# Where the cast of a weight chunk stands in ScalarE's queue at the seams of a two-block network

## The chip, the cores and the metric

One core of one Trainium2 chip. The time is the device time of one execution in microseconds (us); several runs of a kernel are taken and their median stands for it. The profile is of one execution, and its span leaves out a little of what the device time holds.

## The reference

256 tokens of width 1024, in float32, pass through a first block (one layer: a mixer of four branches, a feed-forward) and then a second block of two layers. What matters here is the second block:

```python
def swiglu_ffn(h, w_up, w_down):
    a, b = jnp.split(h @ w_up, 2, axis=-1)
    return (jax.nn.silu(a) * b) @ w_down
...
    for l in range(DEPTH_2):
        x = x + 0.5 * swiglu_ffn(rmsnorm(x, ffn1_norm[l]), ffn1_w_up[l], ffn1_w_down[l])
        x = x + mixer(rmsnorm(x, mix_norm[l]), w_in[l], b_in[l], ..., w_out[l], cos, sin)
        x = x + 0.5 * swiglu_ffn(rmsnorm(x, ffn2_norm[l]), ffn2_w_up[l], ffn2_w_down[l])
        x = rmsnorm(x, final_norm[l])
    return x
```

The feed-forward's hidden width is 2816. The mixer projects its normed input (gated convolution, queries, keys and values, gates), runs windowed attention and a convolution of 31 taps, and projects their gated sum back with w_out. A *seam* below is a place where a part has added its result to x and the next part starts with a norm of x: three seams follow a feed-forward's down projection, two follow w_out.

## The kernel before

**Layout.** Activations lie transposed, 128 channels on the partitions and the 256 tokens along the free axis. The residual x is four tiles `X[0]` to `X[3]`, each a pair of 128-channel columns. Every float32 operand of a matmul is split in two float32r parts: a high half, which is a copy rounded by a cast, and a low half, which is the rest. A product is three matmuls: high by high, high by low, low by high.

**Weights come in chunks** of 128 x 2048 (1 MB; 8 blocks of 128 input channels for a pair of output columns). A down projection has 22 blocks, so each column pair takes chunks of 8, 8 and 6; w_out, the gated convolution (glu) and the up projections take one chunk of 8 for each. `weights(name, i, c0)` fetches a chunk and those after it in a fixed order, up to `ahead` chunks ahead: SP loads the raw chunk (L189), ScalarE casts it to the high half (L195), VectorE subtracts to get the low half (L197). There are two buffers for raw chunks, three for high and three for low halves. TensorE reads the halves in `mm_pair` (L269): a full chunk is 48 matmuls of 256 columns, one of 6 blocks is 36. `mm` sets `ahead` to 2 before each call; its parameter `hold`, which would set it to 1 for the last chunk of a product, is not used by any caller.

**The seam.** After column pair j of a down projection or of w_out, VectorE adds the product to `X[j]` (L482 or L738), and `after(j)` feeds the pair into the next norm. `Norm.feed` multiplies each of the two columns by the norm's gain into its high half on ScalarE (L388, in `split`), takes the low half on VectorE (L389), squares x on ScalarE (L397) and adds the squares on VectorE (L398). At the seam from layer 0 to layer 1 the norm before (`pre`) is applied in the same feed: one more square and two more multiplications (L423) come first. The factor that the norm needs from the sum of squares is multiplied in later (`Norm.done`: a column sum on TensorE in L351, a reciprocal root in small VectorE operations, a broadcast), so the next product's matmuls can start with the column pairs that are there: the first chunk after the seam uses pair 0 first and pair 3 last.

**Order.** The program is traced in the order of the Python code. A planner then puts the instructions of each engine in a fixed queue when the program is built, by its own estimate of when each becomes ready and by their order in the trace; `high_priority` moves a part of the trace forward in that order. Buffers of one name (a tag) are shared, and an instruction that writes a new tile waits for a free one. `issue_after(ins)` ties what it encloses on `ins`'s engine behind `ins` in the queue, without a wait for its end.

Other names in the rows: `mm` is a PSUM tile of a product, `xs` holds the halves of the normed input, `slot` is an arena buffer (the hidden tile of a feed-forward among others), `pc` is the column sum. In the mixer, `zsq` (L579) and `ra` (L594) are tiles of one tag (`t2`, four buffers) around the queries and keys: the code asks for the square of a projected half in its turn, and for `ra` after the last square of a group of heads, with raised priority. Each `ra` is a product of one such half and a table. L683 are the convolution's taps.

Of the kernel before, what the change touches and what calls it, by code (L numbers as in the profile page):

```python
# [1 line left out]

# [1 line left out]

# [16 lines left out]
KD = D // P  # L21
# [111 lines left out]
class Builder:  # L133
    def __init__(self, ctx, tc, dram):
        self.tc, self.nc, self.d, self.ctx = tc, tc.nc, dram, ctx
        pool = lambda n, b=1, **kw: ctx.enter_context(tc.tile_pool(name=n, bufs=b, **kw))
        self.p_raw = pool("raw", 2)
        self.p_hi = pool("hi", 3)
        self.p_lo = pool("lo", 3)
        self.con = pool("con")  # L140
        self.st = pool("st")
        self.ar = pool("ar")
        self.tp = pool("tmp", 2)
        ps = bass.MemoryType.PSUM
        self.p_mm = pool("pmm", 3, space=ps)
        self.p_park = pool("park", 1, space=bass.MemoryType.DRAM)
        self.parked, self.parking = {}, iter(())
        self.p_sm = pool("psm", 1, space=ps)
        self.p_sc = pool("psc", 3, space=ps)
        self.p_y = pool("py", 1, space=ps)  # L150
        self.queue, self.ready = [], {}
        self.twice, self.later = False, iter(())
        self.next_ = 0
        self.ahead = 2
        nc = self.nc
        self.ones = self.con.tile([P, P], F32, name="ones")
        nc.vector.memset(self.ones, 1.0)
        self.eps = self.con.tile([P, 16], F32, name="eps")
        nc.vector.memset(self.eps, EPS)
        self.eps = self.eps[:, :1]  # L160
        self.ident = self.con.tile([P, P], F32, name="ident")
        self.X = [self.st.tile([P, 2, NT], F32, name=f"x{j}") for j in range(4)]
# [6 lines left out]
    def weights(self, name, i, c0=0, first=None):  # L169
        key = (name, i, c0)  # L170
        while key not in self.ready or self.next_ < min(self.ready[key][2] + 1 + self.ahead, len(self.queue)):
            n, ii, cc, w, how = self.queue[self.next_]
            nc = self.nc
            r = self.p_raw.tile([P, CH], F32, name="raw")
            by = (BY_QKV if n[:3] == "qkv" else BY) // 4
            h = self.p_hi.tile([P, CH + 64], F32R, name="hi")[:, by:by + CH]
            lo = self.p_lo.tile([P, CH + 64], F32R, name="lo")[:, by:by + CH]
            if self.next_ < 2:
                for j in range(4):
                    c = slice(j * 512, (j + 1) * 512)  # L180
                    if self.next_ == 0:
                        first(j)
                    nc.sync.dma_start(r[:, c], self.d[n][ii, :, c])
                    nc.scalar.copy(h[:, c], r[:, c])
                    nc.vector.tensor_sub(lo[:, c], r[:, c], h[:, c].bitcast(F32))
                self.ready[n, ii, cc] = (h, lo, self.next_)
                self.next_ += 1
                continue
            nc.sync.dma_start(r[:, :w], self.d[n][ii, :, cc:cc + w])  # L189
            if how == 1:  # L190
                nc.sync.dma_start(lo.bitcast(F32)[:, :w], self.parked[n, ii])
            if how == 2:
                nc.scalar.mul(lo[:, :w], r[:, :w], -1.0)
                nc.gpsimd.dma_start(lo[:, :w], self.d[n][ii, :, cc:cc + w], accum_op=ALU.add)
            self.cast = nc.scalar.copy(h[:, :w], r[:, :w]).ins  # L195
            if how == 0:
                nc.vector.tensor_sub(lo[:, :w], r[:, :w], h[:, :w].bitcast(F32))  # L197
            self.ready[n, ii, cc] = (h, lo, self.next_)
            self.next_ += 1
        h, lo, _ = self.ready[key]  # L200
        next(self.parking, None)
        return h, lo
# [179 lines left out]
    def split(self, src, H, L, gain=None):  # L382
        nc = self.nc
        if gain is None:
            nc.scalar.copy(H, src)  # L385
            return nc.vector.tensor_sub(L, src, H.bitcast(F32))  # L386
        else:
            nc.scalar.mul(H, src, gain)  # L388
            return nc.vector.scalar_tensor_tensor(L, src, gain, H.bitcast(F32), op0=ALU.mult, op1=ALU.subtract)  # L389

    def sumsq(self, acc, x, tag="sqa", bufs=1):
# [16 lines left out]
    class Norm:  # L408
# [6 lines left out]
        def feed(self, j, sums=True):  # L415
            b = self.b
            if j == 0:
                self.H, self.L = b.new_xs()
            x = b.X[j]
            if self.pre:  # L420
                self.acc0 = b.sumsq(self.acc0, x, "zq", 6)
                for i in range(2):
                    b.nc.scalar.mul(x[:, i], x[:, i], b.prm(self.pre, 2 * j + i))  # L423
            for i in range(2):
                k = 2 * j + i
                ins = b.split(x[:, i], self.H[k], self.L[k], b.prm(self.gain, k))
            if sums:
                self.acc = b.sumsq(self.acc, x)
            return ins

# [26 lines left out]
    def ffn(self, l, n, norm, after, duo=False):  # L457
        nc = self.nc
        nk = DFF2 // P
        hid = [self.slot(i, [P, 4, NT], F32R) for i in range((nk + 1) // 2)]  # L460
        H = [hid[k // 2][:, k % 2] for k in range(nk)]
        L = [hid[k // 2][:, 2 + k % 2] for k in range(nk)]
        for m, pt in self.mms(f"{n}u{l}", nk, norm.H, norm.L, duo):
            if m == 0:
                norm.done(duo)
            z = self.t2("z")
            nc.vector.tensor_mul(z, pt, norm.rb2)  # L467
            s = self.t1("s")
            ins = nc.scalar.activation(s, z[:, 0], AF.Silu)
            if m == 4:  # L470
                self.mark = ins.ins
            f = self.t1("f")
            nc.vector.tensor_mul(f, s, z[:, 1])  # L473
            if m == 3:
                self.parking, self.later = self.later, iter(())
            self.split(f, H[m], L[m])
        for j in range(4):
            pt = self.mm(f"{n}d{l}", j, nk, H, L)
            if n == "ffn2" and l == NL - 1 and j == 3:
                after(j, pt)  # L480
                break
            nc.vector.scalar_tensor_tensor(self.X[j], pt, 0.5, self.X[j], op0=ALU.mult, op1=ALU.add)  # L482
            after(j)
# [18 lines left out]
    def mixer(self, l, norm, after):  # L502
        nc = self.nc
        H, L = norm.H, norm.L
# [22 lines left out]
        for m in range(8):  # L527
            pt = self.mm(f"glu{l}", m, KD, H, L)
# [21 lines left out]
        for c in QKV:  # L550
# [4 lines left out]
            for hf in range(2):  # L555
                h, lo = self.weights(f"qkv{l}", 2 * c + hf)
                for j in range(2):
                    for i in range(4):
                        k = hf * 4 + i
                        js = slice(j * P, (j + 1) * P)  # L560
                        w = slice(i * 512, (i + 1) * 512)
# [172 lines left out]
                nc.vector.tensor_add(g[:, 0], g[:, 0], g[:, 1])  # L734
                self.split(g[:, 0], MH[m], ML[m])
        for j in range(4):
            pt = self.mm(f"out{l}", j, KD, MH, ML)
            nc.vector.tensor_add(self.X[j], pt, self.X[j])  # L738
            after(j)

# [587 lines left out]
```

## Time and profile before

| | |
|---|---|
| device time, median of 3 runs | 1812.47 us (1810.83 to 1815.7) |
| the profiled execution: device time | 1818.6 us |
| its span | 1816.7 us |
| TensorE busy | 1765.8 us, 97% |
| VectorE busy | 1390.5 us, 77% |
| ScalarE busy | 932.3 us, 51% |
| GpSimd busy | 84.1 us, 5% |
| mean granted TensorE clock | 0.984 |

Times in rows are us from the start of the span. Engines: PE is TensorE's matmuls, PEld its weight loads, DVE is VectorE, ACT is ScalarE, POOL is GpSimd, SP issues loads. A timeline row shows start, duration, engine, line, operation, output<-inputs, shapes and count (consecutive equal instructions are merged), and in brackets the idle time of the engine before it with what ended it. The granted clock is a share of 2.4 GHz; 0.50 is 1.2 GHz.

### The profile page before, as it was taken

What the parts mean: (1) busy time and instruction counts of PE and PEld (TensorE: products, weight loads), DVE (VectorE), ACT (ScalarE), POOL (GpSimd) and SP (SyncE); (2) the same over time, 40 slices, a digit from 0 to 9 for tenths busy, and PEclk for the clock granted to TensorE, in tenths of its full rate; (3) what the DMA queues carried; (4) which work ended last, traced back from release to release, by engine and by line L of the source; (5) the groups of instructions that cost most, each with busy time, mean ns of one, the idle gap of its engine ahead of it and who ended that gap; (6) DMA issues with size and microseconds to landing.
All of it is one profiled execution on the core that took longest, in us unless ns stands there. A gap on an engine that the chain in (4) does not pass through costs nothing.

```text
span 1816.7 us, 33703 instructions
## 1 busy us (share of the span) xinstructions
PE 1765.8 (97%) x14048; PEld 1694.6 (93%) x14048; DVE 1390.5 (77%) x2137; ACT 932.3 (51%) x1134; POOL 84.1 (5%) x156
## 2 busy tenths in 40 slices
PE   7999999999999999999999999999999999999998
PEld 7989899999999898888999999999998888999997
DVE  7886878656776699998877766777689998776653
ACT  4354455444555454467645555555444456654443
POOL 0000000000011100000000110011300000000000
PEclk9999999999999999999999998999989999999999
DMA  7425447773788758875458986688757774455552
GB/s 280 173 94 209 159 146 272 270 266 135 269 305 302 250 188 295 286 259 141 169 180 276 304 295 218 223 299 299 273 195 286 282 274 142 163 186 186 186 183 96
DMA packets 79560, 409.34 MB, mean 225 GB/s; under 512 B 9905, under 2 KB 10033, under 8 KB 40241
## 3 DMA queue, kind: packets, MB, share of 16 engines
q1 hardware_dynamic: 51552, 339.07, 53.9%
q0 software_dynamic: 10000, 35.66, 5.8%
q10 hardware_dynamic: 17856, 32.48, 4.9%
q8 instruction: 110, 1.80, 0.4%
q14 instruction: 42, 0.34, 0.1%
HBM read 375.71 MB, written 31.46 MB: 224 GB/s over the span
## 4 chain that ended last, share of the span: by engine, by line
PE 48%; DVE 19%; issue 17%; DMA 6%; ACT 5%; POOL 2%; ACTq 0%; POOLq 0%; DVEq 0%
PE mm L269 37%; DVE lo L197 7%; ACT hi L195 3%; DVE spare L683 2%; DMA raw<-ffn1d 2%; DVE slot L683 2%; PE mm L292 1%; PE mm L564 1%; PE mm L562 1%; PE mm L563 1%; PE y L646 1%; DMA raw<-out 1%; POOL qkv L217 1%; DMA raw<-glu 1%; DMA raw<-ffn1u 1%
## 5 line engine op out<-in xcount | busy, mean ns | idle before, releaser
L269 PE MATMUL mm<-xs,hi 128*128 128x256 f32 x5440 | 974.0, 282 | 18.4 <-ACT xs L388 8.6
L269 PEld LDWEIGHTS mm<-xs,hi 128*128 128x128 f32 x5440 | 831.4, 190 | 26.4 <-ACT xs L388 9.2
L195 ACT CAST hi<-raw 128x2048 fp32r<-128x2048 f32 (+1 forms) x288 | 542.6, 1885 | 504.5 <-PE mm L269 235.5
L197 DVE TENSOR_TENSOR lo<-raw,hi 128x2048 fp32r<-128x2048 f32 (+1 forms) x254 | 573.6, 2259 | 292.4 <-ACT hi L195 291.5
L269 PE MATMUL mm<-xs,lo 128*128 128x256 f32 x2720 | 738.7, 282 | 5.8 <-DVE lo L197 5.3
L269 PEld LDWEIGHTS mm<-xs,lo 128*128 128x128 f32 x2720 | 504.6, 190 | 9.4 <-DVE lo L197 6.3
L269 PE MATMUL mm<-slot,hi 128*128 128x256 f32 x2304 | 399.7, 278 | 4.1 <-DVE slot L1010 2.4
L269 PEld LDWEIGHTS mm<-slot,hi 128*128 128x128 f32 x2304 | 345.2, 188 | 5.1 <-DVE slot L1010 2.8
L269 PE MATMUL mm<-slot,lo 128*128 128x256 f32 x1152 | 306.0, 278 | 0.0
L269 PEld LDWEIGHTS mm<-slot,lo 128*128 128x128 f32 x1152 | 209.8, 188 | 0.0
L683 DVE SCALAR_TENSOR_TENSOR slot<-slot,prm,slot 128x256 f32<-128x256 f32 x360 | 149.3, 479 | 0.0
L385 ACT CAST slot<-f 128x256 fp32r<-128x256 f32 (+1 forms) x104 | 45.3, 439 | 159.4 <-DVE f L473 156.9
L562 PE MATMUL mm<-hi,xs 128*128 128x512 f32 x288 | 113.1, 393 | 0.0
L563 PE MATMUL mm<-lo,xs 128*128 128x512 f32 x288 | 113.1, 393 | 0.0
L564 PE MATMUL mm<-hi,xs 128*128 128x512 f32 x288 | 112.6, 391 | 0.0
L562 PEld LDWEIGHTS mm<-hi,xs 128*128 128x128 f32 x288 | 54.1, 188 | 11.0
L467 DVE TENSOR_TENSOR z<-mm,rb 128x512 f32<-128x512 f32 x88 | 60.2, 688 | 5.4 <-ACT rb L379 1.3
L563 PEld LDWEIGHTS mm<-lo,xs 128*128 128x128 f32 x288 | 54.1, 188 | 11.0
L216 DVE TENSOR_TENSOR slot<-slot 128x512 fp32r<-128x512 f32 x96 | 63.9, 685 | 0.5 <-ACT slot L215 0.5
L564 PEld LDWEIGHTS mm<-hi,xs 128*128 128x128 f32 x288 | 54.1, 188 | 11.0
L386 DVE TENSOR_TENSOR slot<-f,slot 128x256 fp32r<-128x256 f32 (+1 forms) x104 | 47.7, 462 | 15.0 <-ACT slot L385 14.8
L215 ACT CAST slot<-slot 128x512 fp32r<-128x512 f32 x96 | 56.5, 610 | 0.0
(283 smaller groups left out, 1422.4 us busy)
## 6 DMA issues: line engine op xcount, KB each, us to landing
raw<-ffn1u SPq DMA_DIRECT2D x44, 1024.0 KB, 5.1
raw<-ffn2u SPq DMA_DIRECT2D x44, 1024.0 KB, 4.8
raw<-qkv SPq DMA_DIRECT2D x36, 1024.0 KB, 6.5
raw<-win SPq DMA_DIRECT2D x24, 1024.0 KB, 4.8
lo<-qkv SPq DMA_DIRECT2D x18, 1024.0 KB, 6.8
raw<-wup SPq DMA_DIRECT2D x16, 1024.0 KB, 4.8
raw<-wdown SPq DMA_DIRECT2D x16, 1024.0 KB, 6.1
raw<-ffn1d SPq DMA_DIRECT2D x16, 1024.0 KB, 6.8
```

Source lines behind the costliest of these rows:

```text
L195: self.cast = nc.scalar.copy(h[:, :w], r[:, :w]).ins
L197: nc.vector.tensor_sub(lo[:, :w], r[:, :w], h[:, :w].bitcast(F32))
L215: nc.scalar.copy(h, r)
L216: nc.vector.tensor_sub(r.bitcast(F32R), r, h.bitcast(F32))
L269: nc.tensor.matmul(pt[:, m], w[:, i, c], x[k], start=first and m == 0 and i == 0 and j == 0, stop=last and i == n - 1 and j == 2, skip_gro ...
L385: nc.scalar.copy(H, src)
L386: return nc.vector.tensor_sub(L, src, H.bitcast(F32))
L467: nc.vector.tensor_mul(z, pt, norm.rb2)
L562: nc.tensor.matmul(pz[j], H[k][:, js], h[:, w], start=k == 0, stop=False)
L563: nc.tensor.matmul(pz[j], H[k][:, js], lo[:, w], start=False, stop=False)
L564: nc.tensor.matmul(pz[j], L[k][:, js], h[:, w], start=False, stop=k == 7)
L683: nc.vector.scalar_tensor_tensor(acc[i], u, w, acc[i], op0=ALU.mult, op1=ALU.add)
```

## The change

At the last chunk of the last column pair (j = 3) of each down projection of the second block and of w_out, `mm` now gets `hold`, so that this call of `weights` runs one chunk ahead and not two. The chunk that it leaves out is then traced by the next call, that of the first chunk behind the seam, which also traces the one after it. `split` notes its last multiplication, `Norm.feed` hands it on at j = 3, and the next cast that `weights` traces is tied behind it in ScalarE's queue; the casts after that one are not tied.

```diff
@@ Builder.__init__
         self.queue, self.ready = [], {}
+        self.fed = None
@@ Builder.weights
-            self.cast = nc.scalar.copy(h[:, :w], r[:, :w]).ins
+            with self.tc.issue_after(self.fed) if self.fed else nullcontext():
+                self.cast = nc.scalar.copy(h[:, :w], r[:, :w]).ins
+            self.fed = None
@@ Builder.split
-            nc.scalar.mul(H, src, gain)
+            self.fed_ = nc.scalar.mul(H, src, gain).ins
@@ Builder.Norm.feed
             if sums:
+                if j == 3:
+                    b.fed = b.fed_
                 self.acc = b.sumsq(self.acc, x)
@@ Builder.ffn
         for j in range(4):
-            pt = self.mm(f"{n}d{l}", j, nk, H, L)
+            pt = self.mm(f"{n}d{l}", j, nk, H, L, j == 3)
@@ Builder.mixer
         for j in range(4):
-            pt = self.mm(f"out{l}", j, KD, MH, ML)
+            pt = self.mm(f"out{l}", j, KD, MH, ML, j == 3)
```

## Rows read from the trace of the kernel before

**Rows 1.** The page, busy us of each engine (share of the span), instructions:

```profile
PE 1765.8 (97%) x14048; PEld 1694.6 (93%) x14048; DVE 1390.5 (77%) x2137; ACT 932.3 (51%) x1134; POOL 84.1 (5%) x156
```

**Rows 2.** Timeline of ScalarE around the seam at 623 us:

```profile
619.28 1.92 ACT L195 CAST hi<-raw 128x2048 fp32r<-128x2048 f32 x1 [1.97 <-DMA raw<-glu]
627.87 1.90 ACT L195 CAST hi<-raw 128x2048 fp32r<-128x2048 f32 x1 [6.67 <-DMA raw<-glu]
629.67 0.90 ACT L388 ACTIVATE xs<-x,prm 128x256 fp32r<-128x256 f32 x2
630.48 0.61 ACT L397 ACTIVATE sq<-x 128x512 f32<-128x512 f32 x1
```

**Rows 3.** Timeline of VectorE around the same seam:

```profile
623.68 0.68 DVE L482 SCALAR_TENSOR_TENSOR x<-mm,x 128x512 f32<-128x512 f32 x1
629.79 2.29 DVE L197 TENSOR_TENSOR lo<-raw,hi 128x2048 fp32r<-128x2048 f32 x1 [5.43 <-ACT hi L195]
632.00 0.88 DVE L389 SCALAR_TENSOR_TENSOR xs<-x,prm,xs 128x256 fp32r<-128x256 f32 x2
```

**Rows 4.** Timeline of TensorE around the same seam:

```profile
626.35 0.40 PE L269 MATMUL mm<-xs,hi 128*128 128x256 f32 x2
...
626.70 0.40 PE L269 MATMUL mm<-xs,hi 128*128 128x256 f32 x2
...
630.23 1.01 PE L269 MATMUL mm<-xs,hi 128*128 128x256 f32 x3 [3.01 <-ACT xs L388]
...
632.54 0.58 PE L269 MATMUL mm<-xs,hi 128*128 128x256 f32 x1 [1.09 <-DVE xs L389]
```

**Rows 5.** Timeline of ScalarE at the seams at 929 and 1119 us:

```profile
929.62 1.91 ACT L195 CAST hi<-raw 128x2048 fp32r<-128x2048 f32 x1 [2.36 <-PE mm L269]
...
1119.52 1.91 ACT L195 CAST hi<-raw 128x2048 fp32r<-128x2048 f32 x1 [2.24 <-DMA raw<-ffn1u]
```

**Rows 6.** Windows: stretch, length, PE busy (instructions), granted clock, DMA share, GB/s:

```profile
629.60:639.80 10.20, 8.48 (x38) 0.50 0.30 103
...
sum 30.70, PE 26.98; mean PE 8.99
```

**Rows 7.** Windows of 22 us from the first matmul behind a seam:

```profile
622.85:644.85 22.00, 17.90 (x119) 0.77 0.49 178
1312.61:1334.61 22.00, 17.97 (x121) 0.77 0.58 200
1116.35:1138.35 22.00, 19.28 (x123) 0.77 0.52 187
929.38:951.38 22.00, 21.68 (x184) 1.00 0.55 188
```

**Rows 8.** Timeline of TensorE at the seams at 1119 and 1314 us:

```profile
1123.34 0.62 PE L269 MATMUL mm<-xs,hi 128*128 128x256 f32 x3 [2.63 <-ACT xs L388]
...
1319.91 1.01 PE L269 MATMUL mm<-xs,hi 128*128 128x256 f32 x3 [2.94 <-ACT xs L388]
```

**Rows 9.** Timeline of VectorE in the mixer, queries and keys:

```profile
692.81 4.44 DVE L683 SCALAR_TENSOR_TENSOR slot<-slot,prm,slot 128x256 f32<-128x256 f32 x11
...
702.47 0.68 DVE L594 TENSOR_TENSOR ra<-zq,slot 128x512 f32<-128x512 f32 x1
```

**Rows 10.** Timeline of ScalarE in the same stretch:

```profile
689.22 0.63 ACT L579 ACTIVATE zsq<-zq 128x512 f32<-128x512 f32 x1 [4.13 <-DVE zq L576]
...
702.48 0.62 ACT L579 ACTIVATE zsq<-zq 128x512 f32<-128x512 f32 x1
```

**Rows 11.** Timeline of TensorE behind the seam at 929 us:

```profile
935.70 0.95 PE L351 MATMUL pc<-ones,sqa 128*128 128x1 f32 x8
```

**Rows 12.** Windows: a stretch of TensorE behind another wait:

```profile
908.00:918.00 10.00, 9.15 (x79) 1.00 0.50 194
```

**Rows 13.** The page, DMA issues: KB each, median us to landing:

```profile
raw<-ffn2u SPq DMA_DIRECT2D x44, 1024.0 KB, 4.8
```

**Rows 14.** The chain that ended last, 600 to 660 us:

```profile
621.59 6.18 DMA raw<-glu
```

More of the change, by code (lines that the diff above doesn't have):

```diff
@@ L1 @@
-from contextlib import ExitStack
+from contextlib import ExitStack, nullcontext
 import numpy as np
```

## Prediction

> **What bounds the kernel now.** I read the page first: TensorE is busy for 97% of the span [rows 1], so only its idle time and its slow clock can be won. The list of waits names what it waits for longest inside the second block: the scaled copy of the residual that ScalarE writes in line 388. The timeline finds three such waits, all at the seams from a feed-forward to what follows (near 623, 1119 and 1314 us); the two seams after the mixer (near 929 and 1618) have the same code without such a wait.
>
> Call the last chunk before a seam C0, the next ones C1 to C5, and E the end of C0's matmuls. ScalarE runs its instructions in the order in which they were queued, and at all five seams the cast of C3 is queued ahead of the feed of the last column pair. At 623 us that cast had to wait 6.67 us for its load, so the two feed multiplications ran at 629.67 [rows 2], although their input, the sum of line 482, was there at 624.36 [rows 3]. TensorE had run 36 matmuls of C1 on the three older pairs, stopped, got the first half of the feed at 630.23 and waited once more, 1.09 us, for line 389 [rows 4], which stood on VectorE behind the subtraction of the same C3 [rows 3]. At 1119 us the cast waited 2.24 us for its load. At 929 its data had come, the feed was late by the cast alone (1.9 us), and 36 matmuls, three of which take 0.35 us, covered that with 4.2 us [rows 4, 5].
>
> The second half of the price is the clock. Behind each of the three long waits the granted clock is 0.50 (1.2 GHz) for 10.2 to 10.3 us, 30.7 in all [rows 6].
>
> **What the three seams cost.** The windows of 22 us from the first matmul of C1 hold 119, 121 and 123 matmuls at the disturbed seams and 184 at the other two, of which one is shown [rows 7]. Short by 65, 63 and 61, at 0.117 us: 7.6 + 7.4 + 7.1 = 22.1 us. Of it 3.01 + 1.09 at the first, 2.94 + the same 1.09 at 1319 and 2.63 are waiting, 10.8 in all [rows 4, 8]; the rest, 11.3, is the clock.
>
> The Trainium skill (TensorE: Matmul & The Clock Gate, section HAM oscillation) charges half of the throttled time: by it 30.7 us would cost 15.3, and with the waits, less the 3.7 us of them that lie inside the slow stretches, the seams would cost 22.4. That hardly differs from the count, and the sum stands on the count.
>
> **The change, part by part.** With hold, the last call for weights of C0 fetches C1 only. The load, cast and subtraction of C2 are then traced behind the feed, and its cast alone is tied behind the feed's last multiplication. This happens five times; at the sixth place (the last feed-forward) no chunk is left and nothing is fed.
>
> *The load of C2* sits on SP, which has loads alone here. It is not tied and needs a raw buffer that C0's subtraction has freed: it goes out as before, and before E its data had come (its cast ran at 619.28 at the first seam [rows 2]). Cost nothing; if something stood ahead of it on SP, that thing's length.
>
> *The cast of C3*, the one that blocks today, is not tied at all. Whether it moves depends on whether its hi buffer may be handed out before C2's, which is asked for earlier. The trace says it may not. The product of line 594 had its operand, as the square of it at 689.22 shows, and a raised priority, yet VectorE ran eleven convolution taps from 692.81 and began it at 702.47, when ScalarE began the square that had asked for a buffer of that tag one place earlier [rows 9, 10]. So I take the buffers of a tag as given in program order: C3 follows C2, and C2 follows the feed.
>
> *The feed* then follows the sum at once: sum 0.68 [rows 3], two multiplications 0.90, the square 0.61 [rows 2]. The high halves are there at E + 1.6, the low ones (0.88 for two [rows 3]) a little later, before TensorE's E + 4.2, and ScalarE is free at E + 2.2. All of the 10.8 us of waiting, and with it the clock's fall, should go. At 1119 the feed has one more square and two more multiplications, as long as these: high halves at E + 3.1, low ones by E + 3.6, still in time.
>
> *What is late next: C2.* Cast from E + 2.2, 1.91 us [rows 5], subtraction 2.29 [rows 3]: done at E + 6.4, at 1119 at E + 7.9. TensorE ends C1 at E + 5.6 (48 matmuls) and wants the low half with C2's third matmul, E + 5.7; the column sum of line 351 (0.95) can run in between, as it is now near that place [rows 11]. Bounds: nothing where the column sum comes first (C2 is then wanted at E + 6.6), 0.7 where it doesn't; I take 0.3 at four seams, 1.2 in all. At 1119 the bounds are 1.2 and 2.2; taken 1.2, since the sum of the older squares can fill the rest. Does such a short wait drop the clock? The nearest row is a stretch of 10 us from 908, in which TensorE is idle for 0.85 and the granted clock stays at 1.00 [rows 12]. I take no clock cost; the other end is the 4.5 us that the clock cost at 1119 (7.1 less 2.63), for each seam.
>
> *C4's load* waits for C2's raw buffer, which is freed at E + 6.4 instead of about E. 4.8 us for a load [rows 13], cast and subtraction 4.2: E + 15.4, wanted at E + 6.6 + 2 x 5.6 = E + 17.8. The 2.4 us to spare hide it: nothing. POOL's queue is not passed.
>
> Sum: 22.1 - 1.2 - 1.2 = 19.7 us. The profiled execution, 1818.6 us, becomes 1798.9. It is 6.1 above the median of the runs shown, and I take the seams to be the same in all: 1812.5 - 19.7 = **1792.8 us**.
>
> **The rivals.** *C4 starves.* The loads of C4 and C5 now start 2.3 us apart, and a load that overlapped with the next one took 6.18 us [rows 14], not 4.8. That eats 1.4 of the 2.4 us, and one more subtraction (2.29) ahead of C4's on VectorE makes it 1.3 late: at five seams 6.5, so 1799. Against it: the load of C3 today overlaps in the same way and only its cast's place hurts. The Trainium skill (DMA: Bandwidth & Descriptors, section Issuing engines are not separate DMA queues) says that transfers in flight interleave on the same sixteen engines. By that both loads of the pair would be late by up to the length of the overlap; the 6.18 us agrees.
>
> *The change doesn't do what it says.* If buffers are not given in order, C3's cast stays ahead of the feed and C2's comes behind both. The three waits stay. At a mixer seam C2's subtraction then queues behind C3's (to 933.9), the feed's halves and sum (1.4) and ends at 937.5, when TensorE wants it at 935.2 to 936: 1.5 to 2.3 us twice, 1816; with the clock's fall there too, 1825. Against it stands the order of lines 594 and 579 [rows 9, 10], though these are of another tag with four buffers.
>
> *Slower, by C2.* The wait for C2's low half takes the place of the one for the feed at all five seams, and takes the clock with it. From there it decides: five times 4.5 and my 2.4 of waiting are 24.9 against 22.1, so 1815; if the waits reach the 2.6 us that cost the clock today, five times 7.1 = 35.5, so 1826. For it: the waits I left in the sum. Against it: the 0.85 us after 908 that cost no clock, and that nothing ready before E + 4.1 stands ahead of the subtraction on VectorE. The Trainium skill (TensorE: Matmul & The Clock Gate, section A second HAM failure mode) tells of a kernel whose clock swung through micro-idles alone. By that the 1815 would come true; no row here shows it.
>
> **How the numbers follow.** My sum as told: 0.74, with 1789 to 1798 as its own range (residual waits of nothing, or of 0.7 four times, 2.2 once and the clock at one seam, within the runs' scatter). C4 starves: 0.10. No effect at the feed: 0.09. C2 takes the wait's place: 0.07. The range 1787 to 1805 holds the first but for surprises and most of the second: about 0.81. The three runs before lie 4.9 us apart, so 0.3% (5.4 us) is about what a measurement can tell from no change. Faster: 0.74, and 0.07 of the starved case. Same: its other 0.03 and 0.04 of no effect. Slower: 0.05 of no effect and the last case's 0.07.
>
> **What would show it.** On ScalarE at each seam: feed, square, cast, cast, in this order, the feed within 1 us of the sum. No wait of TensorE for line 388; granted clock 1.00 through all five; 175 or more matmuls in each of the five windows. Right in kind but mis-sized: a wait for line 197 at E + 5.7, or for a load at E + 18. Wrong: a cast still ahead of the feed, or the clock at 0.50 behind a new wait.

## The result, and the profile after

| | before | after |
|---|---|---|
| device time, median of 4 runs each, same chip | 1811.65 us (1809.67 to 1815.7) | 1796.64 us (1792.25 to 1799.7) |
| ratio, 95% interval | | 0.9893 (0.987 to 0.9916) |
| the profiled execution: device time / span | 1818.6 / 1816.7 us | 1799.7 / 1797.9 us |
| mean granted TensorE clock | 0.984 | 0.994 |

The kernel became faster by 0.84% to 1.3%. On the 1812.5 us that the prediction started from, the interval is 1788.9 to 1797.2 us; forecast were 1792.8. The profiled executions lie 18.9 us apart; the prediction's sum was 19.7, from 1818.6 to 1798.9.

The page's line of the engines (busy us, share of the span, instructions), which answers to [rows 1]:

```profile
PE 1753.4 (98%) x14048; PEld 1682.8 (94%) x14048; DVE 1386.3 (77%) x2137; ACT 932.4 (52%) x1134; POOL 83.5 (5%) x156
```

TensorE's busy time fell by 12.4 us with the same instructions: matmuls that run at half clock are longer. The rest of the gain is idle time.

Seams keep the names of their times in the kernel before; behind the change they come earlier. Lines have moved: the cast is L197, the low half's subtraction L200, the matmul L272, the column sum L354, the broadcast L376, the feed L391 and L392, its square L400, the added squares L401, the sums L487 and L743. The timeline of ScalarE at the seam near 623 us, against [rows 2]:

```profile
623.22 0.91 ACT L391 ACTIVATE xs<-x,prm 128x256 fp32r<-128x256 f32 x2 [3.21 <-DVE x L487]
624.04 0.62 ACT L400 ACTIVATE sq<-x 128x512 f32<-128x512 f32 x1
624.56 1.90 ACT L197 CAST hi<-raw 128x2048 fp32r<-128x2048 f32 x1
628.80 1.90 ACT L197 CAST hi<-raw 128x2048 fp32r<-128x2048 f32 x1 [2.35 <-DMA raw<-glu]
```

Feed, square, C2's cast, C3's cast: so it stands at all five seams. VectorE there, against [rows 3]:

```profile
622.50 0.69 DVE L487 SCALAR_TENSOR_TENSOR x<-mm,x 128x512 f32<-128x512 f32 x1 [0.16 <-PE mm L272]
623.76 0.89 DVE L392 SCALAR_TENSOR_TENSOR xs<-x,prm,xs 128x256 fp32r<-128x256 f32 x2 [0.58 <-ACT xs L391]
...
626.49 2.29 DVE L200 TENSOR_TENSOR lo<-raw,hi 128x2048 fp32r<-128x2048 f32 x1 [1.11 <-ACT hi L197]
```

The feed starts 0.72 us behind the start of the sum (6.0 before). TensorE, against [rows 4]; nothing in it waits for the feed any more, but there is a new wait:

```profile
627.90 0.95 PE L354 MATMUL pc<-ones,sqa 128*128 128x1 f32 x8
628.71 0.48 PE L272 MATMUL mm<-xs,hi 128*128 128x256 f32 x2
630.76 0.50 PE L272 MATMUL mm<-xs,hi 128*128 128x256 f32 x2 [1.57 <-ACT hi L197]
```

TensorE's queue, as the program was built, says which cast that is (`hi_7018` is C2's high half, `hi_7024` C3's):

```
3152 L354 MATMUL pc_7078<-ones_90,sqa_6488 128x1 x4
3153 L272 MATMUL mm_7111<-xs0_6480,hi_7018 128x256 x2
3154 L272 MATMUL mm_7173<-xs0_6480,hi_7024 128x256 x2
3155 L272 MATMUL mm_7111<-xs0_6480,lo_7019 128x256
```

The planner filled the gap before C2's low half with two matmuls of C3, at all five seams. Here C3's load was late (2.35 us of idle time of ScalarE), so C2 waited for C3. The windows of 22 us from the first matmul of C1, against [rows 7] (stretch, length, PE busy (instructions), clock, DMA share, GB/s), and last the one slow stretch that is left, against [rows 6]:

```profile
622.30:644.30 22.00, 20.43 (x162) 0.92 0.48 162
1112.62:1134.62 22.00, 21.55 (x182) 1.00 0.51 189
1301.27:1323.27 22.00, 22.00 (x189) 1.00 0.54 193
923.56:945.56 22.00, 22.00 (x192) 1.00 0.44 162
...
631.40:634.80 3.40, 3.40 (x18) 0.50 0.66 214
```

119, 123 and 121 matmuls became 162, 182 and 189, and at the mixer's seam 184 became 192.

**The price by seam.** A longer measure, worked out from start times in the timeline of VectorE: from the sum of column pair 1 to the eighth product behind the seam, at the three seams behind a feed-forward (us):

| kernel | 623 | 1119 | 1314 | the three against before |
|---|---|---|---|---|
| before | 83.88 | 83.76 | 82.11 | |
| the change | 79.31 | 76.55 | 74.93 | -19.0 |
| again (below) | 77.54 | 75.88 | 74.43 | -21.9 |
| pin_alone | 77.70 | 80.09 | 78.32 | -13.6 |
| cast_early | 77.89 | 77.07 | 73.32 | -21.5 |
| sub_tied | 76.81 | 75.70 | 76.60 | -20.6 |

At the two mixer seams the same measure changed by +0.8 and -1.1 us. Each number is from one execution: the change and again are the same kernel, 2.9 us apart at the three seams, and in_turn's execution, with the lowest ratio below, gave 16.7 there.

### The profile page after: what moved, and what is told of

It reads as the page before. It is cut to its first block, busy times and chain, and to the rows that moved or that the text cites. A ratio compares the mean times of both kernels' runs of the same rounds, so it can differ in the third digit from the quotient of the medians.

```text
span 1797.9 us, 33694 instructions
## 1 busy us (share of the span) xinstructions
PE 1753.4 (98%) x14048; PEld 1682.8 (94%) x14048; DVE 1386.3 (77%) x2137; ACT 932.4 (52%) x1134; POOL 83.5 (5%) x156
## 4 chain that ended last, share of the span: by engine, by line
PE 47%; DVE 19%; issue 18%; ACT 7%; DMA 7%; POOL 1%; ACTq 0%; DVEq 0%; POOLq 0%
PE mm L272 37%; DVE lo L200 6%; ACT hi L197 4%; DMA raw<-ffn2u 3%; DVE spare L688 2%; DVE slot L688 2%; DMA raw<-ffn2d 2%; PE mm L569 1%; PE mm L568 1%; PE mm L567 1%; PE y L651 1%; POOL qkv L220 1%; DMA raw<-out 1%; PE mm L295 1%; DMA raw<-glu 1%
## 5 line engine op out<-in xcount | busy, mean ns | idle before, releaser
L272 PE MATMUL mm<-xs,hi 128*128 128x256 f32 x5440 | 965.9, 280 | 11.0 <-ACT hi L185 5.9
L272 PEld LDWEIGHTS mm<-xs,hi 128*128 128x128 f32 x5440 | 824.8, 189 | 17.6 <-ACT hi L185 5.9
L200 DVE TENSOR_TENSOR lo<-raw,hi 128x2048 fp32r<-128x2048 f32 (+1 forms) x254 | 573.5, 2259 | 288.0 <-ACT hi L197 286.8
L197 ACT CAST hi<-raw 128x2048 fp32r<-128x2048 f32 (+1 forms) x288 | 542.3, 1884 | 457.8 <-PE mm L272 170.3
L272 PE MATMUL mm<-xs,lo 128*128 128x256 f32 x2720 | 735.4, 280 | 4.3 <-DVE lo L200 3.8
L272 PEld LDWEIGHTS mm<-xs,lo 128*128 128x128 f32 x2720 | 501.2, 189 | 7.9 <-DVE lo L200 4.9
L272 PE MATMUL mm<-slot,hi 128*128 128x256 f32 x2304 | 400.5, 278 | 3.9 <-DVE slot L1015 2.4
L272 PEld LDWEIGHTS mm<-slot,hi 128*128 128x128 f32 x2304 | 345.5, 188 | 4.9 <-DVE slot L1015 2.8
L272 PE MATMUL mm<-slot,lo 128*128 128x256 f32 x1152 | 306.7, 279 | 2.1 <-DVE lo L200 1.8
L272 PEld LDWEIGHTS mm<-slot,lo 128*128 128x128 f32 x1152 | 209.9, 188 | 3.1 <-DVE lo L200 3.1
L569 PEld LDWEIGHTS mm<-hi,xs 128*128 128x128 f32 x288 | 54.1, 188 | 11.1
L389 DVE TENSOR_TENSOR slot<-f,slot 128x256 fp32r<-128x256 f32 (+1 forms) x104 | 47.8, 461 | 12.6 <-ACT slot L388 12.4
```

Source lines behind the costliest of these rows:

```text
L272: nc.tensor.matmul(pt[:, m], w[:, i, c], x[k], start=first and m == 0 and i == 0 and j == 0, stop=last and i == n - 1 and j == 2, skip_gro ...
L569: nc.tensor.matmul(pz[j], L[k][:, js], h[:, w], start=False, stop=k == 7)
```

## The experiments

Ratios are to the kernel before on the same chip, with 95% intervals; medians of the kernel before were 1817.4, 1816.1 and 1817.4 us in the three groups of four.

| run | median us | ratio | interval |
|---|---|---|---|
| again | 1795.9 | 0.9877 | 0.9851 to 0.9904 |
| hold_alone | 1816.1 | 0.9996 | 0.9973 to 1.0019 |
| pin_alone | 1803.4 | 0.9923 | 0.9899 to 0.9947 |
| in_turn | 1794.8 | 0.9872 | 0.985 to 0.9894 |
| kept_busy | 1817.4 | 1.0004 | 0.9981 to 1.0026 |
| cast_early | 1793.1 | 0.9876 | 0.9843 to 0.9909 |
| three_seams | 1799.1 | 0.9908 | 0.9878 to 0.9938 |
| two_seams | 1816.2 | 1.0004 | 0.9982 to 1.0026 |
| sub_tied | 1797.7 | 0.9896 | 0.9865 to 0.9927 |
| chain_tied | 1802.4 | 0.9926 | 0.99 to 0.9952 |
| late_3 | 1795.9 | 0.989 | 0.9857 to 0.9923 |
| late_9 | 1808.5 | 0.9953 | 0.9933 to 0.9972 |

**again**: the changed kernel, no edit.

> The changed kernel itself, once more, beside the three that follow. Theory (the feed was late behind the cast of C3, and the change removes that at all five seams): 0.987 to 0.992 of the kernel before, and the trace again with feed, square, cast, cast on ScalarE. If the wait of 1.57 us at the seam near 623 us comes from the order on TensorE's queue (two matmuls of C3 ahead of the first low half of C2), it comes again, longer or shorter with the load of C3. Rival (an accident of one execution): no wait there in this trace.

0.9877. The rows of ScalarE near 623 us:

```profile
625.52 0.91 ACT L391 ACTIVATE xs<-x,prm 128x256 fp32r<-128x256 f32 x2 [5.42 <-DVE x L487]
...
626.86 3.70 ACT L197 CAST hi<-raw 128x2048 fp32r<-128x2048 f32 x2
```

The casts of C2 and C3 run back to back, since C3's load landed 3.5 us behind the sum and not 6.2, and TensorE does not wait at all: 191 matmuls in the window, clock 1.00. Near 1119 us a wait for C3's cast is there in both, 0.42 us in the change and 0.58 here. So the order on TensorE's queue makes the wait possible, and the load of the one execution decides its length: each side was half right.

**hold_alone**

```diff
             if sums:
-                if j == 3:
-                    b.fed = b.fed_
                 self.acc = b.sumsq(self.acc, x)
```

> Only the hold, without the pin: C2 is still traced behind the feed, but nothing ties its cast. Theory: what costs is the place of the casts ahead of the feed on ScalarE, and without the tie both casts, C2's and C3's, are queued ahead of the feed again; the three waits of 2.6 to 3.0 us and the slow clock behind them return, so the time is that of the kernel before, 0.997 to 1.003. Rival (fetching one chunk later is what helps, since it keeps C3 away from the feed): 0.987 to 0.992, as with both.

0.9996, the time that the theory had. ScalarE near 623 us:

```profile
618.89 1.92 ACT L197 CAST hi<-raw 128x2048 fp32r<-128x2048 f32 x1 [1.62 <-DMA raw<-glu]
626.85 1.90 ACT L197 CAST hi<-raw 128x2048 fp32r<-128x2048 f32 x1 [6.04 <-DMA raw<-glu]
628.65 0.91 ACT L391 ACTIVATE xs<-x,prm 128x256 fp32r<-128x256 f32 x2
```

These are [rows 2] again: without the tie the planner puts both casts ahead of the feed, and the hold alone is worth nothing. The waits of this execution, the fastest of twelve (1809.0 us), are smaller in sum than the theory's: 2.46 and 1.58 us near 623, 1.06 near 1119, 0.88 and 1.58 near 1314, with 10.2 us, nothing and 3.4 us at half clock behind them.

**pin_alone**

```diff
-            self.ahead = 1 if hold and k0 + n == nk else 2
+            self.ahead = 1 if hold and k0 + n == nk and False else 2
```

> Only the pin, without the hold: C2 is traced and cast ahead of the feed as in the kernel before, and the cast tied behind the feed is that of C3. Theory: this removes the same three waits, and C2's low half is ready before TensorE wants it, so neither a wait for it nor for C3's cast (1.57 us at 623, with 3.4 us of half clock behind it) is left: 2 to 4 us less than the changed kernel, 0.985 to 0.990 of the kernel before. Rival (C2's cast must be behind the feed as well, since it delays the feed by 1.9 us): the feed is late by 1 us or more at the five seams and the gain is halved, 0.994.

0.9923: 7 to 8 us more than the change, and the theory's 2 to 4 us less was wrong. The feed did follow its sum at once (0.72 us near 623), so the rival's reason was wrong too. VectorE near 1115 us shows what was missed:

```profile
1109.71 2.29 DVE L200 TENSOR_TENSOR lo<-raw,hi 128x2048 fp32r<-128x2048 f32 x1 [1.32 <-ACT hi L197]
1111.92 0.68 DVE L487 SCALAR_TENSOR_TENSOR x<-mm,x 128x512 f32<-128x512 f32 x1
```

C2's subtraction stands ahead of the *sum*. TensorE had begun C1 at 1108.60, so C0's product had been ready for 3.2 us (its last matmul ended at 1108.76). The kernel before has the same: C1 begins 3.2 us ahead of the sum near 1119, 2.3 near 1314 and 0.8 near 623. Its rows of VectorE and TensorE near 1119 us:

```profile
1117.31 2.29 DVE L197 TENSOR_TENSOR lo<-raw,hi 128x2048 fp32r<-128x2048 f32 x1 [2.70 <-ACT hi L195]
1119.52 0.68 DVE L482 SCALAR_TENSOR_TENSOR x<-mm,x 128x512 f32<-128x512 f32 x1
...
1116.35 0.39 PE L269 MATMUL mm<-xs,hi 128*128 128x256 f32 x2
```

In the change C1's first matmul starts 0.2 us ahead of the sum at all five seams. And in pin_alone VectorE near 632 us, with TensorE's rows and the windows behind:

```profile
632.41 2.29 DVE L200 TENSOR_TENSOR lo<-raw,hi 128x2048 fp32r<-128x2048 f32 x1
634.62 0.15 DVE L326 SCALAR_TENSOR_TENSOR na<-na,nv 128x2 f32<-128x2 f32 x1
```

```profile
635.12 0.68 PE L376 MATMUL pb<-ident,rs 128*128 128x128 f32 x4 [2.27 <-DVE rs L328]
1114.66 0.38 PE L272 MATMUL mm<-xs,hi 128*128 128x256 f32 x1 [1.70 <-ACT xs L391]
```

```profile
1115.50:1122.40 6.90, 6.90 (x35) 0.51 0.29 106
1316.90:1320.30 3.40, 3.40 (x19) 0.50 0.78 289
```

C4's subtraction got into the middle of the norm's short chain (operations of 0.16 us), and TensorE waited for the broadcast, 2.27 us here and 2.44 near 1316. New theory: the hold earns its part on VectorE, by keeping those two subtractions off the sum and off the chain. sub_tied and chain_tied test it.

**in_turn**

```diff
...
-            self.mm_pair(pt, h, lo, H, L, range(k0, k0 + n), k0 == 0, k0 + n == nk)
+            self.since = 0 if hold and k0 + n == nk else self.since + 1
+            with self.tc.issue_after(self.last) if self.since == 3 else nullcontext():
+                self.mm_pair(pt, h, lo, H, L, range(k0, k0 + n), k0 == 0, k0 + n == nk)
```

(`self.last` is the last matmul traced.)

> The changed kernel, and at the five seams the matmuls of C3 are tied behind the last one of C2 on TensorE, so that no cast of C3 stands between TensorE and C2. Theory: the wait of 1.57 us at 623 and the half clock behind it go, and TensorE waits for C2's low half by 0.3 us or less: 2 to 3.5 us less than the changed kernel. Rival (C2's low half is what TensorE lacks there, and the two matmuls of C3 only fill the wait): the wait comes in its place for line 200, 0.3 to 0.7 us at each seam, and the time is that of the changed kernel or 1 us more.

0.9872 against 0.9877 for again: the two can't be told apart. TensorE's rows at two seams, and the window behind the second wait:

```profile
628.03 0.28 PE L273 MATMUL mm<-xs,lo 128*128 128x256 f32 x1
...
1113.74 0.40 PE L273 MATMUL mm<-xs,lo 128*128 128x256 f32 x1 [1.11 <-DVE lo L201]
```

```profile
1114.00:1117.40 3.40, 3.40 (x18) 0.50 0.76 263
```

Near 623 us no wait is left. At the seam with the longer feed the wait for C2's low half comes, 1.11 us, and the clock falls for 3.4 us behind it. The theory holds at the one, the rival at the other.

**kept_busy** (from the kernel before)

```diff
...
+                self.mm_pair(pt, h, lo, H, L, range(6), True, False)
+                dummy = self.p_sc.tile([P, 512], F32, name="sc", tag="sc")
+                with self.tc.issue_after(self.last):
+                    for i in range(22):
+                        ins = self.nc.tensor.matmul(dummy[:, :NT], h[:, :P], H[0], start=True, stop=True)
+                with self.tc.issue_after(ins.ins):
+                    self.mm_pair(pt, h[:, 1536:], lo[:, 1536:], H[6:], L[6:], range(2), False, True)
...
```

> The kernel before with its three late feeds, and 22 matmuls of no use (2.6 us at the duration of the others, results unread) queued on TensorE where it waits for the feed: between the 36th matmul of C1 and the first one on the last pair, at the seams near 623, 1119 and 1314 us. Theory (of the 22.1 us that the three seams cost, 10.8 is waiting and 11.3 the slow clock behind it): the waits stay, as busy time, the granted clock stays at 1.00 behind them, and the kernel gains up to 11.3 us, 0.994 of the kernel before; 0.997 if the remaining wait of 1.09 us at two seams still drops the clock there. Rival (the late feed and the late casts set the time, the clock costs little): 0.999 to 1.002.

1.0004: the expected gain of up to 11.3 us did not come. TensorE's rows, and the windows behind them:

```profile
627.87 2.73 PE L287 MATMUL sc<-xs,hi 128*128 128x256 f32 x22
632.40 0.38 PE L270 MATMUL mm<-xs,hi 128*128 128x256 f32 x1 [1.80 <-ACT xs L399]
634.71 0.39 PE L270 MATMUL mm<-xs,hi 128*128 128x256 f32 x1 [1.93 <-DVE xs L400]
...
1124.10 2.73 PE L287 MATMUL sc<-xs,hi 128*128 128x256 f32 x22
1127.10 0.38 PE L270 MATMUL mm<-xs,hi 128*128 128x256 f32 x1 [0.15 <-DVE xs L400]
```

```profile
635.80:642.60 6.80, 6.80 (x35) 0.50 0.35 145
1125.00:1135.00 10.00, 9.85 (x85) 1.00 0.36 114
```

The slow stretches fell from 30.7 to 10.2 us, but the filling did not replace the waits: near 623 TensorE had begun C1 3.2 us ahead of the sum (0.83 in the kernel before), and filling and waits came to 6.3 us against 4.1. Only near 1119 was the wait filled (0.15 us were left) and the clock kept, and there the seam was 2.9 us shorter (80.91 us by the measure above). But there the feed also came earlier, 5.2 us behind C1's first matmul against 6.5 in the kernel before. So the run does not weigh the clock at any of the three seams.

**cast_early**

```diff
...
                 if j == 3:
                     b.fed = b.fed_
+                    b.fetch()
                 self.acc = b.sumsq(self.acc, x)
```

(`fetch` is the body of the loop in `weights`, one chunk.)

> The changed kernel with C2 fetched between the feed and the square: cast and subtraction of C2 come 0.6 to 0.7 us earlier on ScalarE and VectorE, the square and the column sum 1.9 us later, and TensorE's queue has C2's matmuls in turn, without two of C3 among the first. Theory (what is left at the seams is the wait for C2's low half or for C3's cast): no wait over 0.3 us at 623, at most 0.5 near 1112, 1 to 4 us less than the changed kernel, 0.984 to 0.988 of the kernel before. Rival (the column sum and the norm's broadcast behind it become late, as where the pin stood alone): a wait of over 1 us for line 376's input at the seams into the mixer, 0.990.

0.9876, the same as again. The window of 22 us at the seam near 1119 (the other four have 189 matmuls each at 1.00):

```profile
1109.31:1131.31 22.00, 21.41 (x184) 1.00 0.49 174
```

One wait of 0.59 us near 1117 (at most 0.5 was expected), clock 1.00 through all five, no wait for the broadcast. In the trace this is what the prediction meant the change to do; the 1 to 4 us that it could save lie within what the runs can tell.

**three_seams and two_seams**

```diff
-            pt = self.mm(f"out{l}", j, KD, MH, ML, j == 3)
+            pt = self.mm(f"out{l}", j, KD, MH, ML)
-                if j == 3:
+                if j == 3 and b.ahead == 1:
```

(two_seams: the same second edit, with `j == 3` taken from the call in `ffn` instead.)

> The change at the three seams behind a feed-forward alone; the two behind the mixer as before. Theory (the price lay at these three, the feed of the other two was late under cover): the whole gain, 0.985 to 0.991 of the kernel before. Rival (the mixer's seams give a fifth each): 0.992 to 0.994.

> The change at the two seams behind the mixer alone; the three behind a feed-forward as before. Theory: nothing, 0.998 to 1.002 of the kernel before, with the three waits of 2.6 to 3.0 us and the slow clock behind each in the trace. Rival (the mixer's seams give a fifth each, or lose to C2's low half): 0.994 to 0.996, or 1.002 to 1.004.

0.9908 and 1.0004: the gain lies behind the feed-forwards. By the measure above the three seams gave 18.5 us in three_seams, the mixer's two 1.3 us together in two_seams, which also has the three waits and slow stretches of 10 to 14 us again. three_seams has one slow stretch too, near 1117, where TensorE had waited 0.58 us for C3's cast; the rows of TensorE and the window:

```profile
1116.12 0.51 PE L272 MATMUL mm<-xs,hi 128*128 128x256 f32 x2 [0.58 <-ACT hi L197]
...
1117.40:1120.80 3.40, 3.40 (x19) 0.50 0.96 325
```

**sub_tied**

```diff
-            self.ahead = 1 if hold and k0 + n == nk else 2
+            self.ahead = 2
+            self.defer = hold and k0 + n == nk
...
-            if how == 0:
+            if self.defer:
+                self.owed, self.defer = (lo[:, :w], r[:, :w], h[:, :w].bitcast(F32)), False
+            elif how == 0:
...
                     b.fed = b.fed_
+                    if b.owed:
+                        with b.tc.issue_after(ins.ins):
+                            b.nc.vector.tensor_sub(*b.owed)
+                        b.owed = None
```

> The pin without the hold, as in pin_alone, but C2's subtraction alone is traced behind the feed and tied behind the feed's low halves on VectorE; C2's cast stays early. Theory: pin_alone lost against the change because C2's subtraction (2.29 us) stood on VectorE ahead of the sum, which made the feed late by up to 1.9 us, and because C4's subtraction stood inside the norm's short chain, for which TensorE waited 2.27 and 2.44 us. Both are out of the way here: no wait of TensorE over 0.4 us at the five seams, clock 1.00 through them, 0.983 to 0.988 of the kernel before, the same as the change or up to 4 us less. Rival (the hold helps by its loads, which are spread otherwise): as pin_alone, 0.990 to 0.995.

0.9896, 1797.7 us: 5.6 us under pin_alone and, within the intervals, the time of the change; not under it, and over the range that was expected. The intervals of sub_tied and pin_alone overlap, but each of its six runs (1794.8 to 1800.0 us) is shorter than each of pin_alone's (1801.2 to 1809.5), and the kernel before had the same median beside both. The "1.9 us" by which the expectation has the feed late is 3.2 by the rows of pin_alone above. The windows near 623 and 1119, and TensorE's one wait:

```profile
623.20:645.20 22.00, 20.35 (x173) 1.00 0.59 212
1109.31:1131.31 22.00, 22.00 (x191) 1.00 0.46 171
```

```profile
630.72 0.49 PE L358 MATMUL pc<-ones,sqa 128*128 128x1 f32 x3 [1.65 <-DVE sqa L405]
```

Two of the three seams are without any wait (190 matmuls in the third window). Near 623 C2's load landed 0.8 us behind the sum; its cast, ahead of the feed, made the feed late, and the added squares stood behind C2's subtraction. An early cast in front of the feed is a risk whenever its load is late.

**chain_tied** (from pin_alone)

```diff
...
+                with self.tc.issue_after(self.tail) if self.tail else nullcontext():
+                    nc.vector.tensor_sub(lo[:, :w], r[:, :w], h[:, :w].bitcast(F32))
+                self.tail = None
...
```

(`self.tail` is the last operation of the norm's chain.)

> The pin without the hold, as in pin_alone, with the subtraction of the next chunk tied behind the norm's short chain on VectorE. Theory: the two waits of 2.27 and 2.44 us for the broadcast of line 376 go, and the slow clock behind the second; C2's subtraction still stands ahead of the sum, so the wait of 1.7 us and the slow clock near 1115 stay: 3 to 6 us less than pin_alone, 0.988 to 0.991 of the kernel before. Rival (the broadcast's lateness is what the feed's lateness leads to): the waits come back with another name, as pin_alone.

0.9926, as pin_alone. The rival was right: the wait for the broadcast is there as before, 2.20 and 2.19 us:

```profile
638.43 0.68 PE L379 MATMUL pb<-ident,rs 128*128 128x128 f32 x4 [2.20 <-DVE rs L331]
```

The chain is whole now, but it begins behind C3's subtraction, at 636.16, and the planner, which reckons with the shorter chain, put the broadcast 20 matmuls behind the column sum on TensorE's queue, where pin_alone has 38. The wait of 1.7 us near 1115, which the theory left in place, did not come in this execution (no wait there; C2's subtraction ended as C0 did). So tying the chain alone gives nothing; sub_tied, which moves C2's subtraction, has no wait for the broadcast, with 28 matmuls in between. Which of its two effects, the sum's or the broadcast's, is worth how much is not settled by these two runs.

**late_3 and late_9** (from sub_tied, at the three seams)

```diff
+            junk = b.p_sc.tile([P, 2, NT], F32, name="sc", tag="sc") if j == 3 and b.lag else None
+            for _ in range(b.lag if j == 3 else 0):
+                junked = b.nc.scalar.copy(junk, x).ins
...
-                ins = b.split(x[:, i], self.H[k], self.L[k], b.prm(self.gain, k))
+                with b.tc.issue_after(junked) if junk is not None else nullcontext():
+                    ins = b.split(x[:, i], self.H[k], self.L[k], b.prm(self.gain, k))
...
-                self.acc = b.sumsq(self.acc, x)
+                with b.tc.issue_after(b.fed_) if junk is not None else nullcontext():
+                    self.acc = b.sumsq(self.acc, x)
```

> sub_tied, and at the three seams behind a feed-forward ScalarE makes three copies of no use (128x512, 0.6 us each) between the sum and the feed. Theory (TensorE has 4.2 us of matmuls on the older pairs from about the time of the sum, and a feed that is late by less costs nothing): the feed's high halves are there at the sum + 3.1 us, no wait at the two seams into the mixer, 0.3 to 0.6 us at the third, where the feed is 1.5 us longer; within 2 us of sub_tied. Rival (each microsecond of a late feed is paid): 5 to 6 us more than sub_tied.

> The same with nine copies: the feed comes about 5.5 us behind the sum, as late as in the kernel before, though no cast and no load stands ahead of it. Theory (10.8 us of waits and 11.3 us of clock were the price of the lateness alone): waits of about 2 us at two seams and 3.5 us at the third, granted clock 0.50 for about 10 us behind each, 17 to 24 us more than sub_tied, about the time of the kernel before. Rival A (only the waits cost): 7 to 9 us more. Rival B (the late load of C3 and its cast cost by themselves, not through the feed): 0 to 4 us more.

late_3: 0.989, the time of sub_tied. ScalarE near 623 us has the feed 1.8 us later, and the only wait for it is one of 0.19 us near 1120 (there are others: 2.16 and 0.80 us for a cast whose load was late, 1.04 and 0.39 us for a low half):

```profile
626.71 1.83 ACT L434 COPY sc<-x 128x512 f32<-128x512 f32 x3 [1.04 <-DVE x L501]
628.48 0.91 ACT L396 ACTIVATE xs<-x,prm 128x256 fp32r<-128x256 f32 x2
```

late_9: 0.9953, 10.8 us more than sub_tied. ScalarE and TensorE at the three seams, and the windows behind:

```profile
623.51 5.57 ACT L434 COPY sc<-x 128x512 f32<-128x512 f32 x9 [1.01 <-DVE x L501]
629.01 0.90 ACT L396 ACTIVATE xs<-x,prm 128x256 fp32r<-128x256 f32 x2
```

```profile
629.57 0.90 PE L276 MATMUL mm<-xs,hi 128*128 128x256 f32 x2 [2.17 <-ACT xs L396]
632.29 0.50 PE L276 MATMUL mm<-xs,hi 128*128 128x256 f32 x2 [0.65 <-ACT hi L199]
...
1118.17 1.10 PE L276 MATMUL mm<-xs,hi 128*128 128x256 f32 x2 [3.10 <-ACT xs L396]
...
1312.02 0.91 PE L276 MATMUL mm<-xs,hi 128*128 128x256 f32 x2 [2.38 <-ACT xs L396]
```

```profile
629.50:639.50 10.00, 9.14 (x72) 1.00 0.53 206
1118.00:1128.00 10.00, 9.83 (x48) 0.55 0.55 204
```

(The third seam is like the first: 1.00.)

A feed that is late by itself brings waits back, 7.7 us for the feed at the three seams and 0.65 twice for C3's cast behind it, so Rival B falls. But the clock fell behind the longest alone, for 10.2 us. The 10.8 us are outside both ranges, nearer to Rival A's 7 to 9 than to the theory's 17 to 24. That the clock always doubles the price of a late feed was wrong. Counted from C1's first matmul the feed starts as late here (6.7, 8.0 and 6.4 us) as in the kernel before (6.8, 6.5 and 6.8), yet the kernel before takes 8.9 us more, and its profiled execution has three slow stretches to one here. The stretch above has 48 matmuls in 10 us and kept_busy's window at 1.00 has 85; 37 matmuls are 4.3 us, so two such stretches would make 8.7 (an estimate). The clock may thus be what is left, but no run sets it apart.

## Why the prediction was right

**The price of the seams, 22.1 us: right.** again gives back 21.9 at the three seams, cast_early 21.5, the profiled execution of the change 19.0, that of in_turn 16.7.

**Its halves: the waits right, the clock not settled.** TensorE's idle time in the 22 us behind the three seams fell from 10.8 to 2.0 us. What else the seams gave back must be the clock, since the same windows at 1.00 have 182 to 192 matmuls. But the direct test failed (kept_busy), and late_9 shows waits of 2.2 and 2.4 us without a slow stretch: 11.3 us was the clock's price in executions like that of [rows 6], not a fixed price of a wait.

**Queue order, and buffers in program order: right.** C3's cast stands behind C2's, and C2's behind the feed, at all five seams. hold_alone shows that the tie is what moves them. That C3's cast follows because buffers of a tag are given in program order fits this, but no run tests that reason by itself.

**The feed at once: right, with a cause missed.** "The feed then follows the sum at once", and its high halves were at the sum + 1.6 us. But the prediction took the sum itself as standing at E and the move of C2 as a mere cost. In the kernel before C2's subtraction held the sum up at these seams: it started 0.8, 3.2 and 2.3 us behind C1's first matmul, 0.2 in the change. Moving C2 behind the feed took that away too. pin_alone, which leaves C2 in front, gave 13.6 us at the three seams, and sub_tied, which moves its subtraction as well, 20.6. The total was right because it was counted from matmuls in windows and not from the chain of one cast. That the edit also freed the sum was luck: by the prediction's own chain, late cast to late feed, pin_alone would have given as much.

**What is late next: right in size, wrong in place.** C2's low half was done 6.28 us behind the sum (E + 6.4 forecast) and 7.74 near 1119 (7.9). The wait was not for line 197's low half but for C3's cast, two of whose matmuls the planner had put ahead of it: 1.57 and 0.42 us in the profiled run, 0.58 in again, against 2.4 forecast. "I take no clock cost" was wrong for the 1.57: 3.4 us at half clock, 162 matmuls instead of 175 or more. By the prediction's own list, the clock at 0.50 behind a new wait was a sign of being wrong; it came at one seam of five. Forecast 1.2 near 1119 with C2 in turn, measured 1.11 (in_turn).

**C4's load: right.** Its buffer came free at the sum + 6.31 us (E + 6.4; near 1119 + 7.8) and the load took 4.7 to 4.8 us at the three seams in the change and in again, so it landed at + 11.1 (near 1119 + 12.5). In again its low half was done at + 15.9 (near 1119 + 17.0) against E + 15.4 forecast. C4 did not starve. The Trainium skill (DMA: Bandwidth & Descriptors, section Issuing engines are not separate DMA queues) has loads in flight interleave; in again C5's, which started 2.2 us after C4's near 623, took 5.7 us and C4's 4.8. So it was at four of the five seams there, where only the later of the pair paid; near 929 C4's took 6.1 us and C5's 6.9, and both did.

**The rivals.** C3's cast ahead of the feed all the same, and C2's low half with the clock at five seams: neither came in the change. The second is seen small in in_turn, at one seam. The Trainium skill (TensorE: Matmul & The Clock Gate, section A second HAM failure mode) tells of micro-idles that alone make the clock swing; here one single wait under 1 us at a seam had a slow stretch behind it, the 0.58 us in three_seams with 3.4 us; the others (0.32 to 0.80 us, in seven runs) had none.

**The sum: right.** 19.7 forecast; the ratios 0.9893 and 0.9877 make it 19.4 and 22.3 us of 1812.5.

## What to carry to other kernels

When an in-order engine holds an early, optional job (a cast whose data may be late) ahead of a late, urgent one, look at every engine that the job runs on: here the cast of one chunk delayed the feed on ScalarE and the subtraction of the chunk before it delayed the sum on VectorE, and undoing the first alone gave two thirds. Count the price of a seam from the work that the bounding engine did in a fixed window, not from the one wait that the list names. And look at what the planner puts into the gap that is left: two matmuls of the next chunk tied this one to the next one's load.

## What the runs showed that was not expected

Whether the clock falls behind a wait of TensorE, and for how long, varies wherever the longest single wait is 2.46 us or less. From the traces of these runs, waits at a seam from 0.4 us on (two close together as a sum; in kept_busy the filling lies ahead of them) and the slow stretch behind them:

| wait, us | run | slow stretch, us |
|---|---|---|
| 0.42 to 0.80 | the change, again, in_turn, kept_busy, cast_early, three_seams, late_3 | none |
| 0.58 | three_seams | 3.4 |
| 1.04, 1.06 | late_3, hold_alone | none |
| 1.11 | in_turn | 3.4 |
| 1.57 | the change | 3.4 |
| 1.65 | sub_tied | none |
| 1.70 | pin_alone | 6.9 |
| 2.16 | late_3 | 6.8 |
| 2.19 / 2.20 | chain_tied | 3.4 / none |
| 2.27 / 2.44 | pin_alone | none / 3.4 |
| 2.17 + 0.65, 2.38 + 0.65 | late_9 | none |
| 0.88 + 1.58 | hold_alone | 3.4 |
| 2.46 + 1.58, 2.01 + 1.54 | hold_alone, two_seams | 10.2 |
| 3.10 | late_9 | 10.2 |
| 1.80 + 1.93, 0.79 + 1.93 | kept_busy | 6.8, 3.4 |
| 2.63, 3.01 + 1.09, 2.94 + 1.09 | before | 10.2 to 10.3 |
| 3.52, 3.74 + 1.09 | two_seams | 13.7 |

Behind each of the six single waits of 2.63 us and more the clock stood at 0.50 for 10.2 us or longer; below that a gain that rests on the clock could not be counted on in these runs. The times of one kernel go with it: of the 17 runs of the kernel before beside again, the fastest (1809.8 us) had a mean granted clock of 0.990 and the slowest (1824.4 us) 0.985.
